# Forgetting attention with a hybrid short convolution: score tiles with keys on partitions in place of transposing P

## The chip, the cores and the metric

The kernel runs on one core of a Trainium2 chip. The time is the device time of one execution in microseconds. Three runs of the kernel before took 593.88, 595.31 and 597.03 us; their median is 595.31.

## The reference

One layer on 1040 positions (16 meta tokens and 1024 real ones), width 1024. A normalised input goes through one projection, whose columns are q, k, v (8 heads of 64 each), a forget logit per head, a gate z, and four groups of 512 columns for a gated convolution. The attention is what the change touches:

```python
log_f = jax.nn.log_sigmoid(f_logit + b_f)
cum_logf = jnp.cumsum(log_f, axis=1)
s = einsum('bqhd,bkhd->bhqk', q, k) * DH ** -0.5
s = s + c_query - c_key                      # c is cum_logf of the head
s = jnp.where(key_pos <= t, s, -inf)
p = softmax(s, axis=-1)
attn = einsum('bhqk,bkhd->bqhd', p, v)
y_attn = group_rmsnorm(attn, attn_norm_g, 8) * silu(z_attn)
y_conv = group_rmsnorm(gate_b * conv3(gate_c * xc), conv_norm_g, 8) * silu(z_conv)
out = rmsnorm(h + concat(y_attn, y_conv) @ w_out)
```

`group_rmsnorm` divides each head by the root of its mean square plus EPS.

## The kernel before

All matmuls are in fp32r. A float32 operand is split into a leading part (a cast to fp32r) and the rest (a subtraction), and a product is summed from leading x leading, leading x rest and rest x leading.

The program has three parts. First come q, k and v for all heads and the cumulative log-forget gates; q, k (each as leading part and rest), v and the gates' negative sums go to DRAM (`qd`, `kd`, `vd`, `cd`). Then comes the attention loop, with the other projections woven in. Last comes the output projection (L788) with the final norm.

The attention loop has 17 stages, -1 to 15 (L716). Stage g computes the scores for one half c (512 queries) of a head, and finishes the half whose scores the stage before made. Per head the half c=1 comes first, then c=0, so even stages finish c=1 (9 key tiles of 128, the last of 16 keys) and odd stages finish c=0 (5 key tiles).

- **`load_head`** (L576) brings q1, q2, k1, k2, v2 of a head into one of two sets of buffers. q1 holds q's leading part above its rest, k1 the leading part of k twice, q2 the leading part and two rows of ones, k2 the rest of k and the two rows of the gates.
- **`s_step`** (L597) takes 128 queries on the partitions and a piece of keys on the columns (`SCH`, 14 pieces per head), in two matmuls, L605 with K=128 and L606 with K=66. VectorE takes the negated maximum of the piece (L612, or L609 with the causal mask on the last piece); ScalarE writes the exponential to `pn` in SBUF with the sum beside it (L613).
- **`s_end`** (L616) combines the pieces' maxima and sums on POOL, ScalarE and VectorE into factors, and POOL scales all of P in SBUF (L635).
- **`t_step`** (L638) makes one key tile of P with keys on the partitions: up to four 128x128 transposes on TensorE into `pt` (L645), a small VectorE transpose for a corner of 32 (L649, L651), a ScalarE cast to `ph` (L654) and a VectorE subtraction to `pl` (L115).
- **`v_step`** (L662), three key tiles behind (`V_LAG`), multiplies `ph` and `pl` with v2 into `po` (L669). `fold` (L672) adds its two halves into `o`; `norm` (L402) normalises and gates.

What sets the order: each step has a place between 0 and 1 in its stage (`S_AT`, `T_AT`, `V_END`), the stage is sorted by place, and `weave` (L745) puts projection blocks (`block_steps`, three matmuls on L165 a step) between the steps in proportion to their estimated length. The matmuls of the loop are pinned: TensorE runs them in exactly this order. The other engines' instructions are ordered by a scheduler at build time. All loads and stores go through SyncE's queue, in order. Tiles of a pool with `bufs=n` rotate over n buffers, and a new tile waits until the old one's readers are done.

## Time and profile before

| | us |
|---|---|
| median of three runs | 595.31 |
| the profiled execution | 596.83 |
| its span in the profile | 595.1 |
| TensorE busy with matmuls | 578.0 (97% of the span, 3230 matmuls) |
| TensorE's weight loads | 509.6 (86%) |
| VectorE | 377.9 (64%) |
| ScalarE | 285.4 (48%) |
| POOL | 168.0 (28%) |
| chain that ended last | 71% TensorE, 10% DMA, 6% VectorE, 4% POOL, 3% ScalarE |

The busy time of a matmul includes time in which the next one already runs, so the sum of durations is not the time that a group of matmuls takes. The attention loop's scores begin at 167.7 us, its first transposes of P at 185.8 us and its last product with V at 490.9 us; the output projection begins at 493.8 us. The profile's PE is TensorE, DVE VectorE, ACT ScalarE, SP SyncE and its queue SPq.

### The profile page before, as it was taken

The numbers are of one execution on the slowest core, as the hardware profiler recorded it, in microseconds if no ns is written. First come the engines' busy times: TensorE is split into PE (matmuls) and PEld (weight loads), VectorE is DVE, ScalarE is ACT, GpSimd is POOL, SyncE is SP. The second block draws the span as 40 slices with busy tenths as digits, with TensorE's granted clock in tenths as the row PEclk, the third lists the DMA queues.
The fourth block names the chain that finished last, engine by engine and source line by source line (L and its number), as shares of the span: only waits on it lengthen the run. The fifth ranks groups of instructions, "written<-read, shape, count | busy, mean of one in ns | idle before, by whom it ended". The sixth has DMA issues, their size and how long they took to land.

```text
span 595.1 us, 9156 instructions
## 1 busy us (share of the span) xinstructions
PE 578.0 (97%) x3230; PEld 509.6 (86%) x3230; DVE 377.9 (64%) x834; ACT 285.4 (48%) x667; POOL 168.0 (28%) x290
## 2 busy tenths in 40 slices
PE   9999999999998999999999999999999999899995
PEld 6888999999997889988879997889998887688884
DVE  5415851133367686879776888868869777947432
ACT  5355431131044575556764655747636676705221
POOL 1002010121027244151243254430552416710000
PEclk9999999999999999999999999999999999899999
DMA  8764594249811605415126134251350227453201
GB/s 287 237 194 141 195 341 142 70 147 280 262 39 36 144 35 135 120 57 155 44 75 143 71 108 112 75 143 37 111 197 16 73 88 243 171 205 113 100 35 70
DMA packets 35221, 78.14 MB, mean 131 GB/s; under 512 B 4024, under 2 KB 13384, under 8 KB 35176
## 3 DMA queue, kind: packets, MB, share of 16 engines
q1 hardware_dynamic: 35032, 77.57, 41.6%
q8 instruction: 25, 0.41, 0.3%
q14 instruction: 20, 0.16, 0.1%
q10 hardware_dynamic: 144, 0.00, 0.0%
HBM read 55.92 MB, written 21.64 MB: 130 GB/s over the span
## 4 chain that ended last, share of the span: by engine, by line
PE 71%; DMA 10%; DVE 6%; POOL 4%; ACT 3%; issue 3%; SPq 2%; POOLq 0%; ACTq 0%; DVEq 0%
PE pj L165 30%; PE ps L324 8%; PE p L788 8%; PE pt L645 5%; PE po L669 5%; PE pj L788 4%; PE ps L165 4%; DMA k<-kd 3%; DMA ht<-in_h 3%; PE pn L605 3%; PE pn L606 3%; DMA xs<-in_hT 2%; DVE mlo L115 2%; POOL pn L635 1%; DMA wm<-in_w_m 1%
## 5 line engine op out<-in xcount | busy, mean ns | idle before, releaser
L165 PE MATMUL pj<-xhi,wmhi 128*128 128x512 f32 (+1 forms) x384 | 144.9, 377 | 1.0 <-DVE kf L275 0.5
L165 PE MATMUL pj<-xhi,wmlo 128*128 128x512 f32 (+1 forms) x384 | 137.1, 357 | 0.0
L165 PE MATMUL pj<-xlo,wmhi 128*128 128x512 f32 (+1 forms) x384 | 136.8, 356 | 0.0
L613 ACT ACTIVATE pn<-pn,nmx 128x328 f32<-128x328 f32 (+6 forms) x112 | 60.5, 541 | 52.7 <-DVE nmx L612 27.9
L165 PEld LDWEIGHTS pj<-xhi,wmlo 128*128 128x128 f32 x384 | 72.2, 188 | 8.4
L165 PEld LDWEIGHTS pj<-xhi,wmhi 128*128 128x128 f32 x384 | 72.6, 189 | 6.2 <-issue 1.4
L165 PEld LDWEIGHTS pj<-xlo,wmhi 128*128 128x128 f32 x384 | 72.8, 190 | 3.8
L654 ACT CAST ph<-pt 128x512 fp32r<-128x512 f32 (+4 forms) x112 | 49.6, 445 | 51.0 <-PE po L669 23.3
L635 POOL TENSOR_SCALAR pn<-pn,fc 128x328 f32<-128x328 f32 (+4 forms) x112 | 69.3, 639 | 1.6
L115 DVE TENSOR_TENSOR pl<-pt,ph 128x512 fp32r<-128x512 f32 (+1 forms) x96 | 54.6, 572 | 20.2 <-ACT ph L654 19.5
L112 POOL TENSOR_SCALAR wmhi<-wm 128x1024 fp32r<-128x1024 f32 x24 | 26.2, 1093 | 141.2 <-DMA wm<-in_w_m 81.8
L645 PE MATMUL pt<-ident,pn 128*128 128x128 f32 x288 | 47.4, 273 | 3.9 <-POOL pn L635 2.2
L645 PEld LDWEIGHTS pt<-ident,pn 128*128 128x128 f32 x288 | 36.3, 140 | 14.4 <-POOL pn L635 3.6
L115 DVE TENSOR_TENSOR wmlo<-wm,wmhi 128x1024 fp32r<-128x1024 f32 x24 | 29.4, 1223 | 18.0 <-POOL wmhi L112 17.9
L609 DVE CUSTOM_DVE_ANT_0 pn<-pn,maskn 128x328 f32<-128x328 f32 (+3 forms) x64 | 31.9, 500 | 11.0 <-PE pn L606 9.3
L669 PE MATMUL po<-ph,v 128*128 128x512 f32 (+4 forms) x112 | 37.0, 336 | 0.0
L605 PE MATMUL pn<-k,q 128*128 128x328 f32 (+6 forms) x112 | 36.6, 328 | 0.1
L606 PE MATMUL pn<-k,q 66*128 66x328 f32 (+6 forms) x112 | 36.1, 322 | 0.0
L669 PE MATMUL po<-pl,v 128*128 128x512 f32 (+1 forms) x96 | 33.2, 350 | 0.0
L788 PE MATMUL p<-whi,mlo 128*128 128x512 f32 (+1 forms) x77 | 30.2, 392 | 2.4 <-DVE mlo L115 2.4
L165 PE MATMUL ps<-xhi,wmhi 128*128 128x346 f32 (+1 forms) x96 | 31.0, 323 | 1.1 <-ACT qraw L240 1.1
L612 DVE TENSOR_REDUCE nmx<-pn 128x1 f32<-128x346 f32 (+4 forms) x48 | 24.8, 521 | 9.6 <-PE pn L606 9.6
(227 smaller groups left out, 1229.5 us busy)
## 6 DMA issues: line engine op xcount, KB each, us to landing
wm<-in_w_m SPq DMA_DIRECT2D x24, 512.0 KB, 3.8
k<-kd SPq DMA_DIRECT2D x24, 260.0 KB, 5.3
q<-qd SPq DMA_DIRECT2D x24, 256.0 KB, 5.9
vd<-vv SPq DMA_DIRECT2D x9, 512.0 KB, 2.9
v<-vd SPq DMA_DIRECT2D x8, 576.0 KB, 6.5
ht<-in_h SPq DMA_DIRECT2D x8, 512.0 KB, 5.6
yd<-gy SPq DMA_DIRECT2D x16, 256.0 KB, 2.8
q<-in_w_o SPq DMA_DIRECT2D x8, 512.0 KB, 4.5
```

The costliest lines, as they stand in the source:

```text
L115: nc.vector.tensor_tensor(lo, src, f(hi), ALU.subtract)
L165: ins = nc.tensor.matmul(ps[:, :w], wt[:, k, :], xt[:, t0:t0 + w], start=(k == 0 and n == 0), stop=(k == KT - 1 and n == 2))
L324: nc.tensor.matmul(ps[c][:P if n == P else 48, :260], x[k][:, ts_] if n == P else x[:, k, :], w[k][:, 260 * c:260 * c + 260], start=(k == ...
L605: pinned(nc.tensor.matmul(ps[:, :w], q1[:, qs], k1[:, ks], start=True, stop=False))
L606: pinned(nc.tensor.matmul(ps[:, :w], q2[:DH + 2, qs], k2[:DH + 2, ks], start=False, stop=True))
L609: nc.vector.tensor_tensor_reduce(ps[:, :w], ps[:, :w], maskn[:, MASKW - w:], op0=ALU.add, op1=ALU.min, scale=-1.0, scalar=-NEG, accum_out= ...
L613: nc.scalar.activation(pn[j][:, ks], ps[:, :w], AF.Exp, bias=nmx[c][at], scale=-1.0 if last else 1.0, accum_out=smx[c][at])
L635: nc.gpsimd.tensor_scalar(pn[j][:, k0:k0 + w], pn[j][:, k0:k0 + w], fc[:, j % 4, i:i + 1], 1.0, ALU.mult, ALU.mult)
L645: pinned(nc.tensor.transpose(pt[:, q0:q0 + P], pn[j][:, ks], ident))
L654: nc.scalar.copy(ph[:, at:], pt[:, at:])
L669: pinned(nc.tensor.matmul(po[:, at:], v2[:, vk, :], t[:, at:], start=(kt == 0 and i == 0), stop=(kt == 4 * c + 4 and i == len(parts) - 1)))
L788: ins = nc.tensor.matmul(held[n][:, :w], a[:, tt], b[:, cs], start=(e == ORDER[0] and i == 0), stop=(e == ORDER[-1] and i == 2))
```

## The change

Per half of a head the maxima now come from one matmul (K=66: leading part of q times leading part of k, plus the gates), and nothing else is made from those scores. `s_end` takes the maximum over the pieces and splits it into two parts; a new `s_row` turns these into a row (transpose on TensorE, ScalarE copy, DMA to `md` in DRAM, DMA back into two rows of q1). `t_step` computes the scores again, this time all terms, with keys on the partitions and queries on the columns: k2 holds the leading part and the rest of k, q2 the rest and the leading part of q (K=128, L665), and k1 times q1 adds leading x leading, the gates and the negated maximum (K=68, L666). The causal mask is a minimum with `maskt` in PSUM (L670), the exponential goes to `pf` in SBUF, and cast and subtraction read `pf`. P isn't normalised: POOL adds up the tiles `pf` in a running sum (L686), `fold` adds the sum's halves, and `norm` gets the sum over keys with two matmuls and adds its square, times EPS, to the mean square. PSUM goes from three buffers for `pn` and two for `pt` to two and three. The build sets a smaller scratch area for DMA descriptors.

Of the diff, the parts below; imports, comments and the unused lines of the old code are left out.

```diff
+    md = [dram.tile([8, P], F32, name=f"md{i}") for i in range(2 * HEADS)]
...
+    maskt = const.tile([P, P], F32, name="maskt")
...
-    psn = cp.enter_context(tc.tile_pool(name="psn", bufs=3, space=PSUM, reuse_waits="tile"))
-    pst = cp.enter_context(tc.tile_pool(name="pst", bufs=2, space=PSUM, reuse_waits="tile"))
+    psn = cp.enter_context(tc.tile_pool(name="psn", bufs=2, space=PSUM, reuse_waits="tile"))
+    pst = cp.enter_context(tc.tile_pool(name="pst", bufs=3, space=PSUM, reuse_waits="tile"))
...
-    def norm(y, g, z, res):
+    def norm(y, g, z, res, s=None):
...
+        if s is not None:
+            th = own.tile([P, 512], F32R, name="gth")
+            tl = own.tile([P, 512], F32R, name="gtl")
+            nc.scalar.copy(th, s)
+            lo_vec(tl, s, th)
...
         def rest():
+            if s is not None:
...
+                pinned(nc.tensor.matmul(pd, blk, th, start=True, stop=False))
+                pinned(nc.tensor.matmul(pd, blk, tl, start=False, stop=True))
+                d2 = own.tile([P, 512], F32, name="gd2")
+                nc.scalar.activation(d2, pd, AF.Square, scale=DH * EPS ** 0.5)
...
+                nc.vector.tensor_add(res, pm, d2)
+                nc.scalar.activation(res, res, AF.Ln)
...
+    ROW = 0.12
...
-        nc.gpsimd.memset(f(q2[DH:DH + 2, :]), 1.0)
+        nc.gpsimd.memset(f(q1[DH:DH + 4, :]), 1.0)
+        nc.gpsimd.memset(f(k1[DH:DH + 4, :]), 1.0)
         nc.sync.dma_start(f(q1[0:DH]), qd[m][0, es, :])
         nc.sync.dma_start(f(k1[0:DH]), kd[m][0, es, :])
...
     def s_step(hd, j, i):
...
-        pinned(nc.tensor.matmul(ps[:, :w], q1[:, qs], k1[:, ks], start=True, stop=False))
-        pinned(nc.tensor.matmul(ps[:, :w], q2[:DH + 2, qs], k2[:DH + 2, ks], start=False, stop=True))
+        pinned(nc.tensor.matmul(ps[:, :w], q1[:DH + 2, j * P:j * P + P], k1[:DH + 2, k0:k0 + w],
+                                start=True, stop=True))
...
-        nc.scalar.activation(pn[j][:, ks], ps[:, :w], AF.Exp, bias=nmx[c][at], scale=-1.0 if last else 1.0,
-                             accum_out=smx[c][at])
...
-    def s_end(c):
+    def s_end(c, box):
         mx = pnp.tile([P, 4], F32, name="mx")
         nc.vector.tensor_reduce(mx, nmx[c], AX.X, ALU.min)
...
+        box["mx"] = pnp.tile([P, 8], F32R, name="mx2")
+        nc.vector.tensor_copy(box["mx"][:, 0:4], mx)
+        lo_vec(box["mx"][:, 4:8], mx, box["mx"][:, 0:4])
...
+    def s_row(hd, c, box):
+        ps = psn.tile([P, 512], F32, name="pn")
+        pinned(nc.tensor.transpose(ps[:8, :P], f(box["mx"]), ident))
+        mr = pnp.tile([8, P], F32, name="mr")
+        nc.scalar.copy(mr, ps[:8, :P])
+        nc.sync.dma_start(md[2 * hd + c], mr)
+        q1 = heads[hd][0]
+        nc.sync.dma_start(f(q1[DH + 2:DH + 4, 512 * c:512 * c + 512]),
+                          md[2 * hd + c].rearrange("(r j) p -> r (j p)", r=2))
...
+    def t_step(hd, c, kt, box):
...
-            pinned(nc.tensor.transpose(pt[:, q0:q0 + P], pn[j][:, ks], ident))
...
+        pinned(nc.tensor.matmul(pt[:rs.stop, a0:], k2[:, ks], q2[:, qs], start=True, stop=False))
+        pinned(nc.tensor.matmul(pt[:rs.stop, a0:], k1[:DH + 4, ks], q1[:DH + 4, qs], start=False, stop=True))
+        pf = pp.tile([P, 512], F32, name="pf" if kt else "ps", bufs=3 if kt else 2)
+        if kt >= 4 * c:
+            new = pt[rs, a0:min(at + P, 512)]
+            nc.vector.tensor_tensor(new, new, maskt[rs.start:rs.stop, a0 - at + r0:a0 - at + r0 + new.shape[-1]], ALU.min)
+        nc.scalar.activation(pf[rs, a0:], pt[rs, a0:], AF.Exp)
...
+            nc.scalar.copy(ph[:, a0:], pf[:, a0:])
+            lo_vec(pl[:, a0:], pf[:, a0:], ph[:, a0:])
...
+        if kt == 0:
+            box["sum"] = pf
+        else:
+            nc.gpsimd.tensor_tensor(box["sum"][rs, a0:], box["sum"][rs, a0:], pf[rs, a0:], ALU.add)
...
     def fold(hd, c, box):
...
+        nc.scalar.copy(tmp[a], box["sum"][b])
+        nc.gpsimd.tensor_tensor(sums[m, c][a], box["sum"][a], tmp[a], ALU.add)
...
+            steps.append((hi + ROW, 0.0, lambda hd=hd, c=c, mbox=mbox: s_row(hd, c, mbox)))
```

The order moves at three places. The first is TensorE at the end of stage -1, where the first key tile of head 0 begins. L605 and L606 are the two old score products, L645 the transposes of P, L165 (L170 in the change) the projection, L646 the new row transpose, L626 the new score product, L665 and L666 the two products of a key tile. Before:

```order
L165 MATMUL pj<-xlo_112,wmhi 128x512
L165 MATMUL pj<-xhi_111,wmlo 128x512
L605 MATMUL pn<-k_1634,q_1632 128x272 [waits Activation_49]
L606 MATMUL pn<-k_1635,q_1633 128x272
L645 MATMUL pt<-ident,pn_1623 128x128 [waits Pool_49]
L645 MATMUL pt<-ident,pn_1622 128x128
```

Changed:

```order
L170 MATMUL pj<-xhi_132,wmlo 128x512
L646 MATMUL pn<-ident,mx_1869 8x128 [waits DVE_49]
L626 MATMUL pn<-k_1643,q_1641 128x144
L626 MATMUL pn<-k_1643,q_1641 128x272 [waits Activation_49]
L170 MATMUL pj<-xhi_134,wmhi 128x512
L170 MATMUL pj<-xlo_135,wmhi 128x512
L170 MATMUL pj<-xhi_134,wmlo 128x512
L665 MATMUL pt<-q_1642,k_1644 128x512 [waits DMAHW3_49,DMAHW4_49,DMAHW1_49,DMAHW0_49]
L666 MATMUL pt<-q_1641,k_1643 128x512 [waits DMAHW4_49]
```

Where the transposes waited for POOL, the second product of the first key tile now waits for a DMA, with six matmuls between it and the row transpose.

The second is SyncE's queue at the first change of head. `md3` is the row of head 1, half c=1; q1_1918 is q1 of head 1, q1_2332 and k1_2334 belong to head 2, whose buffers head 0 leaves. Changed:

```order
L138 DMA wm_2382<-in_w_m 128x1024 [waits DMAHW5_49,DMAHW0_49,DVE_49]
L610 DMA q2_2333<-qd1_64 64x1024 [waits PE_49]
L649 DMA md3_76<-mr_2291 8x128 [waits Activation_49]
L607 DMA q1_2332<-qd1_64 64x1024 [waits DMAHW7_49,DMAHW4_49,PE_49]
L608 DMA k1_2334<-kd1_68 64x1040
L651 DMA q1_1918<-md3_76 2x512 [waits DMAHW2_49]
L609 DMA k1_2334<-cd_72 2x1040 [waits Pool_49]
```

The row's way out and back (L649, L651) has loads of head 2 before and between, and these wait for TensorE. Two more of the seven changes of head have two large loads between the two as well.

The third is VectorE beside POOL in the finish of one half. L120 is `lo_vec`, L670 the mask, L438 and L439 the norm. VectorE, changed:

```order
L670 TENSOR_TENSOR pt<-pt,maskt 128x128 [waits PE_49]
L438 TENSOR_TENSOR gy<-gy,cv 128x512 [waits Activation_49]
L439 SCALAR_TENSOR_TENSOR gy<-gy,gct,zc 128x512 [waits DVE_49]
L120 TENSOR_TENSOR pl<-pf,ph 128x272 [waits Activation_49]
L670 TENSOR_TENSOR pt<-pt,maskt 128x128 [waits PE_49]
L120 TENSOR_TENSOR pl<-pf,ph 128x144 [waits Activation_49]
```

POOL, changed (L686 the running sum, L714 the fold, L674 a memset, L117 the cast of a weight tile):

```order
L117 TENSOR_SCALAR wmhi<-wm 128x1024 [waits DMAHW2_49,PE_49,Pool_49]
L686 TENSOR_TENSOR ps<-ps,pf 128x512 [waits Activation_49,Pool_49] x3
L686 TENSOR_TENSOR ps<-ps,pf 128x400 [waits Activation_49,Pool_49]
L686 TENSOR_TENSOR ps<-ps,pf 128x272 [waits Activation_49,Pool_49]
L686 TENSOR_TENSOR ps<-ps,pf 128x144 [waits Activation_49,Pool_49]
L674 MEMSET ph 128x16 [waits DVE_49,PE_49]
L686 TENSOR_TENSOR ps<-ps,pf 16x16 [waits Activation_49,Pool_49]
L714 TENSOR_TENSOR osum<-ps,stmp 64x512 [waits Pool_49]
```

The subtractions read `pf` and `ph`; POOL's additions read the same `pf` and the running sum, one for each key tile but the first.

## Rows read from the trace of the kernel before

**Rows 1.** Windows view: busy time and count per engine, granted clock, DMA share.

```profile
190.00:490.00 300.00, 297.25 (x1663) 261.14 (x1661) 232.65 (x575) 179.71 (x456) 109.59 (x203) 1.00 0.33 96
```

**Rows 2.** TensorE's timeline: start, duration, line, operation, output<-inputs, shapes, count.

```profile
186.97 0.60 PE L645 MATMUL pt<-ident,pn 128*128 128x128 f32 x4
187.32 0.47 PE L165 MATMUL pj<-xhi,wmhi 128*128 128x512 f32 x1
187.63 0.39 PE L165 MATMUL pj<-xlo,wmhi 128*128 128x512 f32 x1
187.86 0.39 PE L165 MATMUL pj<-xhi,wmlo 128*128 128x512 f32 x1
```

**Rows 3.** The same, end of prologue; in brackets idle time, its releaser.

```profile
182.93 0.23 PE L605 MATMUL pn<-k,q 128*128 128x144 f32 x1
...
183.10 0.44 PE L165 MATMUL pj<-xhi,wmhi 128*128 128x512 f32 x1
...
183.84 0.28 PE L605 MATMUL pn<-k,q 128*128 128x272 f32 x1
183.97 0.28 PE L606 MATMUL pn<-k,q 66*128 66x272 f32 x1
185.76 0.66 PE L645 MATMUL pt<-ident,pn 128*128 128x128 f32 x4 [1.51 <-POOL pn L635]
```

**Rows 4.** The same view, a product of 32 columns.

```profile
205.23 0.22 PE L669 MATMUL po<-ph,v 128*128 128x32 f32 x1
205.30 0.48 PE L165 MATMUL pj<-xhi,wmhi 128*128 128x512 f32 x1
```

**Rows 5.** Waits of the weight loads: us in total, times, longest.

```profile
PEld pt L645 <- POOL pn L635: 3.6, 4, 1.7
```

**Rows 6.** The page's groups: busy us, mean ns | idle before, releaser.

```profile
L645 PE MATMUL pt<-ident,pn 128*128 128x128 f32 x288 | 47.4, 273 | 3.9 <-POOL pn L635 2.2
...
L115 DVE TENSOR_TENSOR wmlo<-wm,wmhi 128x1024 fp32r<-128x1024 f32 x24 | 29.4, 1223 | 18.0 <-POOL wmhi L112 17.9
...
L606 PE MATMUL pn<-k,q 66*128 66x328 f32 (+6 forms) x112 | 36.1, 322 | 0.0
```

**Rows 7.** DMA issues: count, size, median us from issue to landing.

```profile
yd<-gy SPq DMA_DIRECT2D x16, 256.0 KB, 2.8
...
out<-q SPq DMA_DIRECT2D x6, 256.0 KB, 2.3
```

**Rows 8.** SyncE's timeline: an issue among other loads, one by itself.

```profile
196.18 0.59 SPq L586 DMA_DIRECT2D k<-kd  x1
...
513.85 0.33 SPq L692 DMA_DIRECT2D yd<-gy  x1
```

**Rows 9.** TensorE's timeline, output projection: the longest wait.

```profile
517.21 0.59 PE L788 MATMUL p<-whi,mlo 128*128 128x512 f32 x1 [2.11 <-DVE mlo L115]
```

**Rows 10.** Windows view, the 3.7 us behind that wait.

```profile
517.20:520.90 3.70, 3.69 (x9) 2.92 (x10) 3.70 (x2) 0.96 (x2) 3.70 (x2) 0.54 0.74 262
```

**Rows 11.** POOL's timeline at the start of the output projection.

```profile
490.98 2.60 POOL L552 TENSOR_TENSOR wlo<-q,whi 128x1024 fp32r<-128x1024 f32 x1 [12.60 <-ACT whi L549]
493.54 3.38 POOL L552 TENSOR_TENSOR v<-q,whi 128x1024 fp32r<-128x1024 f32 x1
```

**Rows 12.** VectorE's timeline in the same stretch.

```profile
491.88 2.78 DVE L115 TENSOR_TENSOR mlo<-k,mhi 128x1024 fp32r<-128x1024 f32 x1 [0.57 <-ACT mhi L549]
494.69 0.69 DVE L478 TENSOR_TENSOR zs<-pj,rbc 128x512 f32<-128x512 f32 x1
495.30 2.71 DVE L115 TENSOR_TENSOR mlo<-k,mhi 128x1024 fp32r<-128x1024 f32 x1
```

**Rows 13.** Groups by line and shape: busy us, mean ns | idle, releaser.

```profile
L115 DVE TENSOR_TENSOR pl<-pt,ph 128x512 fp32r<-128x512 f32 x48 | 32.9, 686 | 14.2 <-ACT ph L654 14.0
...
L654 ACT CAST ph<-pt 128x512 fp32r<-128x512 f32 x48 | 27.8, 582 | 18.4 <-PE po L669 10.6 <-PE pt L645 7.8
...
L115 DVE TENSOR_TENSOR gsl<-gy,gsh 128x512 fp32r<-128x512 f32 x16 | 13.0, 812 | 4.0 <-ACT gsh L407 3.9
```

More of the change, by code (lines that the diff above doesn't have):

```diff
@@ L565, in hybrid_kernel @@
     FAST = 0.5
-    pn = [pnp.tile([P, (j + 1) * P + 32], F32, name=f"pn{j}") for j in range(8)]
-    nmx, smx = [], []
+    nmx = []
     for c in range(2):
         nmx.append(pnp.tile([P, 4, 3], F32, name=f"nmx{c}"))
-        smx.append(pnp.tile([P, 4, 3], F32, name=f"smx{c}"))
         nc.gpsimd.memset(nmx[c], -NEG)
-        nc.gpsimd.memset(smx[c], 0.0)
     def load_head(hd):
@@ L597, in s_step @@
     def s_step(hd, j, i):
-        q1, q2, k1, k2, _ = heads[hd]
+        q1, _, k1, _, _ = heads[hd]
         c = j // 4
@@ new lines, in t_step @@
+    def t_step(hd, c, kt, box):
+        q1, q2, k1, k2, _ = heads[hd]
+        end = kt == 4 * c + 4
+        at = kt * P - NM - 512 * c
+        a0 = max(at, 0)
+        qs = slice(512 * c + a0, 512 * c + 512)
+        r0 = DH if end and c == 0 else 0
+        rs = slice(r0, r0 + NM) if end else slice(0, P)
+        ks = slice(kt * P - r0, kt * P + (NM if end else P))
+        pt = pst.tile([P, 512], F32, name="pt")
+        pinned(nc.tensor.matmul(pt[:rs.stop, a0:], k2[:, ks], q2[:, qs], start=True, stop=False))
[5 more added lines that the diff above has]
+        nc.scalar.activation(pf[rs, a0:], pt[rs, a0:], AF.Exp)
+        ph = pp.tile([P, 512], F32R, name="ph")
+        if end:
+            nc.gpsimd.memset(f(ph[:, a0:]), 0.0)
+            nc.scalar.copy(ph[rs, a0:], pf[rs, a0:])
+            lo_vec(ph[r0 + 32:r0 + 32 + NM, a0:], pf[rs, a0:], ph[rs, a0:])
+            box[kt] = a0, 8, (ph,)
+        else:
+            pl = pp.tile([P, 512], F32R, name="pl")
+            nc.scalar.copy(ph[:, a0:], pf[:, a0:])
+            lo_vec(pl[:, a0:], pf[:, a0:], ph[:, a0:])
+            box[kt] = a0, kt, (ph, pl)
+        if kt == 0:
+            box["sum"] = pf
+        else:
+            nc.gpsimd.tensor_tensor(box["sum"][rs, a0:], box["sum"][rs, a0:], pf[rs, a0:], ALU.add)
@@ L681, in fold @@
         nc.vector.tensor_tensor(o[a, 512 * c:512 * c + 512], po[a], tmp[a], ALU.add)
+        if (m, c) not in sums:
+            sums[m, c] = own.tile([P, 512], F32, name="osum", bufs=3)
+        tmp = own.tile([P, 512], F32, name="stmp")
+        nc.scalar.copy(tmp[a], box["sum"][b])
+        nc.gpsimd.tensor_tensor(sums[m, c][a], box["sum"][a], tmp[a], ALU.add)
     def attn_finish(m, c):
@@ L687, in go @@
             y = own.tile([P, 512], F32, name="gy", bufs=2)
-            rest = norm(outs[m, "o"][:, cs], gat[:, m:m + 1], zsil[m][:, cs], y)
+            rest = norm(outs[m, "o"][:, cs], gat[:, m:m + 1], zsil[m][:, cs], y, sums.pop((m, c)))
             def end():
@@ L702, in finish_soon @@
             attn_finish(*soon.pop(0))
-    for j in range(8):
-        nc.gpsimd.memset(pn[j][:, (j + 1) * P + NM:], 0.0)
     def spread(steps, todo, lo, hi):
```

68 lines of the change are left out of this document (20 added, 48 removed).

## Prediction

> **What bounds the kernel now.** I read the busy shares first, then TensorE's own order in time, then who it waits for, then the engines that would take over. In the stretch from 190 to 490 us, which is the attention loop, TensorE is busy 297 of 300 us and VectorE, the next engine, 233 [rows 1]. Busy time of pipelined matmuls says little by itself, so I go by the distance from one start to the next. Full-width projection matmuls start 0.23 us apart, and four transposes take 0.35 us and push the matmul behind them 0.08 further out, so 0.107 each [rows 2]. Two score products of 144 columns take 0.17 together and one of 272 takes 0.13 [rows 3]; one of 32 columns takes 0.07 [rows 4]. Columns and starts therefore set the pace, with few gaps: the weight loads of the transposes waited for POOL's scaling 3.6 us in all [rows 5], 1.5 of it at the very first one, at 184 us [rows 3]. TensorE is the bound. VectorE has 67 idle microseconds in those 300, and POOL 190 [rows 1].
>
> **The change, TensorE's own work.** Per head both versions sweep 4736 columns of scores, in 14 pieces, 338 columns on average, which is 0.16 us a piece between the prices of 272 and 512 columns.
> - The second product of the row-wise scores goes: 112 x 0.16 [rows 6] = -17.9.
> - The transposes of P go: 288 x 0.107 [rows 2, 6] = -30.8.
> - Added are two products for each key tile. Each head has six of 512 columns, two each of 400, 272, 144 and 16. With 0.185 for 400 (between 272 and 512), 0.085 for 144 and 0.07 for 16 (the row of 32 columns), that is 2.34 us, times two products, times 8 heads = +37.4.
> - The products with V lose 16 columns in the narrow tiles: -0.6. The norm's new matmuls, 8 x 2 x 0.23 = +3.7. Sixteen row transposes at 0.107 = +1.7.
>
> Sum: -6.5 us. "No transposes" saves little because the transposes were cheap and are replaced by a second full set of scores.
>
> **Waits that go.** No matmul waits for POOL's scaling of P any more: -3.6 [rows 5].
>
> **The wait that comes: the row of maxima.** The maximum crosses from queries on partitions to a row through a transpose on TensorE, a ScalarE copy, a DMA to DRAM and a DMA back into q1. The second product of the first key tile reads that row, its place on TensorE is fixed, and all projection matmuls queue behind it. The trace of before has no such pair of small transfers. Its bounds are the fastest and a typical write, 2.3 and 2.8 us to landing [rows 7], each twice, with 0.33 to issue each [rows 8] and 0.3 for transpose and copy: 5.5 to 6.5, and I take 6.0. What TensorE has to do meanwhile I counted from the new order with the distances above. In the prologue it is two score pieces, three projection matmuls and one product: 1.2 us. At the seven changes of head (SyncE's piece of the order shows one) it is 4.8 to 6.3, 5.25 on average. At the eight changes inside a head it is about 10 us, which covers it; if SyncE is held up there by 4 us, that cover is gone too.
> - Prologue: 6.0 - 1.2 = +4.8 (between 4.3 and 5.3). After the 2.1 us wait at 517 us [rows 9] the granted clock was 0.54, the lower level of 1.2 GHz, and nine matmuls took 3.7 us [rows 10], 0.41 each in place of 0.23: another +1.6.
> - Changes of head: 7 x 0.75 = 5.3. In three of them SyncE first issues two large loads, held until TensorE is done with the old head, between the write and the read of the row. Each such issue takes 0.59 [rows 8], so 3 x 1.2 = 3.5 more. Together +8.8, between 0 (chain of 4.8, or gaps that other stalls widen) and 7 x 3 = 21 (the read waits behind the data of those loads too).
>
> **VectorE and POOL.** VectorE loses 64 small transposes and 64 memsets (about 23 us) and 16 reciprocals (3), and gains 80 masks of up to 128 columns (about 21), sixteen full operations in the norm (11) and the splits of the maxima (6): +12 on 233, still inside its idle time. ScalarE trades its accumulator reads for copies and squares, about even, at 180 of 300. POOL trades 112 scalings for 96 adds, and it has room. The danger is that the two meet. POOL's add of 1024 columns takes 2.6 us, and up to 3.4 when VectorE works beside it [rows 11]. A VectorE subtraction with both inputs in SBUF took 2.78 and 2.71 beside it [rows 12], against 1.22 without it [rows 6]; the operation between them, which reads PSUM and one SBUF tile, took its usual 0.69 [rows 12]. Today's 96 subtractions that split P read PSUM and one SBUF tile. In the change they read pf and ph, both in SBUF, just when POOL adds the same pf.
>
> What this costs VectorE is bounded by two rows. The norm's subtraction, both inputs in SBUF, took 0.81 beside POOL's scalings, against 0.69 for today's split [rows 13]: 0.12 x 96 = 12 us. At the other end, from 491.9 to 498.0 two subtractions took 5.49 for 2.45 of work, an excess of half the time that POOL was adding. POOL's adds are 29.7 thousand columns and the folds 8.2, at 2.5 ns a column 96 us, so 48 us. I take the 12, the nearest case (512 columns, in this loop), and let half of it reach TensorE, since the maxima and the projection outputs queue behind a stalled subtraction and have two PSUM buffers each: +6, with 0 and 48 as ends.
>
> The Trainium skill, page "SBUF — State Buffer", section "Who interferes with whom", says that a VectorE instruction with two SBUF inputs contends with a GpSimd instruction that reads SBUF, and that the one that comes second is blocked for the whole instruction. By that rule the trace agrees [rows 11, 12], and a subtraction ready 0.58 after its exponential [rows 13] would wait out the rest of a 1.2 us add, 0.6 x 48 = 29 us for the full tiles alone; with half of it on TensorE the sum below would be 8 us higher.
>
> Costed at nothing: the loads of a head, eight transfers as before and a stage ahead of their use; the memsets for them, one more per head, which wait on POOL until TensorE has left the old head, with adds behind them; and the fifth to eighth load for the output projection, which now wait for the last scores of head 7. The work on the first two tile pairs, fetched earlier, covers these; without it one such transfer shows.
>
> **Sum.** The profiled execution took 596.8 us: 596.8 - 6.5 - 3.6 + 4.8 + 1.6 + 8.8 + 6.0 = 607.9. It ran 1.5 above the median of the runs, so **606 us**, 1.8% slower.
>
> **Rivals.**
> - *The row comes in time and the adds hide* (faster). If write and read take 4.5 us, the seven changes of head cost nothing; VectorE's 67 idle microseconds swallow its excess. For it: VectorE idles 14 us before the full-width splits alone, waiting for ScalarE's casts [rows 13], so some slack is there. Against it: the write lands no faster than 2.3 in any row. It decides at 4.8 us for the chain. Time: 596.8 - 10.1 + 3.3 + 1.6 - 1.5 = 590; without the prologue's wait and the clock behind it 585.
> - *VectorE becomes the bound.* With 48 us of excess it needs 233 + 12 + 48 = 293 of 300; if half of its idle time stays, because it waits for others, the loop takes 327, 27 more: 596.8 - 10.1 + 6.4 + 27 - 1.5 = 619, and with every change of head at 3 us 640. For it: each split meets its own add. Against it: POOL is idle two thirds of the time, so adds do not pile up.
> - *It cancels* (no change). The changes of head cost half, the adds nothing: 596.8 - 10.1 + 6.4 + 4.4 - 1.5 = 596. This is also where the time lies if the new products merely take the place of the old ones.
>
> **How the numbers follow.** The forecast has 0.44, the faster rival 0.26, VectorE as the bound 0.14, cancelling 0.16. A measurement of this kernel tells about 0.5% (3 us) from no change. So faster is 0.26, same 0.16, slower 0.58. The range of 586 to 626 takes in all of the middle, most of the faster rival and the lower part of VectorE's; the forecast by itself is 599 to 616.
>
> **What would show it.** Right: the first product with the row waits 4 to 6 us for a DMA near 182 us and the clock drops behind it; several waits of 1 to 3 us at the changes of head; splits of 512 columns above 0.9 us on average; TensorE's distances unchanged. Wrong: no DMA waits on TensorE after the prologue, splits at 0.69, a loop shorter than 300 us (the faster rival); or VectorE busy above 280 of 300 with the waits on its maxima (the second rival).

## The result and the profile after

The changed kernel takes **651.26 us** (median of four runs, 650.38 to 651.84) against 595.19 for the kernel before (593.88 to 597.03): a ratio of 1.094, 95% interval 1.091 to 1.097. The forecast was 606, with 626 as the upper end. The sign was right; instead of the +11 us it is +56. One of the four runs of u_vecsums below, 623.67 us, was a slow one (1.8% above the fastest), and its median is that of the other three.

The busy times, the span and the mean clock of the profiled execution:

```profile
PE 589.5 (91%) x3086; PEld 507.2 (78%) x3086; DVE 424.6 (65%) x818; ACT 290.1 (45%) x587; POOL 199.9 (31%) x226
core 0: 650.0 us, clock 0.978
```

The same stretch of the loop as in [rows 1], with the columns span, TensorE, weight loads, VectorE, ScalarE, POOL, clock, DMA share and GB/s:

```profile
190.00:490.00 300.00, 260.66 (x1308) 221.73 (x1306) 236.13 (x468) 154.78 (x323) 127.93 (x133) 0.96 0.28 80
```

VectorE is busy 236 of 300 us, after 233 before, and POOL 128 after 110; neither is near full. TensorE is emptier, 261 after 297. What TensorE waited for from 150 us to the end (reason: total us, times, longest):

```profile
PE pn L646 <- DVE mx L120: 15.1, 8, 5.0
PE pt L666 <- DMA q<-md: 7.6, 4, 2.6
PE po L695 <- DVE ph L120: 7.4, 7, 1.7
PE pj L430 <- ACT gd L428: 6.1, 5, 3.3
PE pj L170 <- DVE gy L435: 3.3, 2, 2.9
PE pj L431 <- DVE gsl L120: 2.8, 1, 2.8
...
PE pm L430 <- ACT gd L428: 1.7, 2, 1.0
...
PE po L695 <- DVE pl L120: 0.7, 2, 0.4
```

The kernel before has about 7 us of such waits there, none longer than 2.1. Adding up TensorE's distances beyond the prices of [rows 2 to 4] gives 79 us of waits and slow stretches after, 22 before; its own work, priced alike, is 8 us less. That makes +57 - 8 = 49 of the 55 us between the two profiled executions; the other 6 lie in distances too small to count one by one.

Of the 79 us, 52 are the waits of this view (with the lines that are not shown) and some 10 are matmuls at the lower level of TensorE's clock. The granted clock is 0.50 in five stretches before the end, at 228, 283, 385, 478 and 512 us, 27 us together. Four of them come right behind a wait of TensorE (2.61, 2.77, 3.28 and 2.50 us), and the one at 385 begins in a wait of 5.00; behind the wait of 3.51 at 360 us there is none. In the columns of above:

```profile
385.40:392.20 6.80, 4.56 (x13) 3.69 (x14) 4.39 (x7) 1.69 (x5) 1.95 (x2) 0.50 0.02 6
```

The waits have three roots. The row of maxima: 15.1 at its transpose, 7.6 at its transfer. The norm: 6.1 and 1.7 for ScalarE's square of the denominators, 2.8 for the split of the squares, 3.3 for a buffer that the norm holds. And splits of P, above all the 16-column end tile: 7.4.

VectorE's operations by shape (count | busy us, mean ns | idle before):

```profile
L120 DVE TENSOR_TENSOR pl<-pf,ph 128x512 fp32r<-128x512 f32 x32 | 39.7, 1247 | 5.8 <-ACT ph L680 5.8
L120 DVE TENSOR_TENSOR wmlo<-wm,wmhi 128x1024 fp32r<-128x1024 f32 x18 | 28.2, 1564 | 7.7 <-POOL wmhi L117 7.7
L120 DVE TENSOR_TENSOR pl<-ps,ph 128x512 fp32r<-128x512 f32 x16 | 10.9, 684 | 4.4 <-ACT ph L680 4.3
L640 DVE CAST mx<-mx 128x4 fp32r<-128x4 f32 x16 | 5.1, 320 | 0.2
```

The split of P into `pl` takes 1247 ns where POOL adds beside it, and 684 for the first key tile (`ps`), which POOL does not add. The split of the weights takes 1564 in place of 1223 [rows 6].

One place shows how these join, VectorE from 382 us (start, length, instruction):

```profile
382.20 0.15 DVE L638 TENSOR_REDUCE mx<-nmx 128x4 f32<-128x12 f32 x1
382.28 1.27 DVE L483 SCALAR_TENSOR_TENSOR cv<-cx,cwt,cv 128x1024 f32<-128x1024 f32 x1
383.47 1.23 DVE L640 CAST mx<-mx 128x4 fp32r<-128x4 f32 x1
...
384.81 1.27 DVE L484 SCALAR_TENSOR_TENSOR cv<-cx,cwt,cv 128x1024 f32<-128x1024 f32 x1
386.00 1.51 DVE L120 TENSOR_TENSOR pl<-pf,ph 128x512 fp32r<-128x512 f32 x1
387.44 0.15 DVE L120 TENSOR_TENSOR mx<-mx,mx 128x4 fp32r<-128x4 f32 x1
```

POOL in the same stretch, and TensorE behind it (the last bracket is idle time and its releaser):

```profile
383.13 1.54 POOL L686 TENSOR_TENSOR ps<-ps,pf 128x512 f32<-128x512 f32 x1 [3.72 <-ACT pf L671]
385.63 1.33 POOL L686 TENSOR_TENSOR ps<-ps,pf 128x400 f32<-128x400 f32 x1 [0.97 <-ACT pf L671]
```

```profile
387.64 0.37 PE L646 MATMUL pn<-ident,mx 128*8 128x128 f32 x1 [5.00 <-DVE mx L120]
388.67 0.63 PE L170 MATMUL pj<-xhi,wmhi 128*128 128x512 f32 x1
389.10 0.63 PE L170 MATMUL pj<-xlo,wmhi 128*128 128x512 f32 x1
```

The maximum of a half (L638) is ready at 382.3. Its cast of four columns (L640), 0.15 to 0.17 us in twelve of the sixteen halves, takes 1.23: it ends as POOL's addition ends. Two convolution steps of 1.2 us and one blocked split of 1.5 stand between, and the rest (the second `mx`) comes at 387.5. TensorE, at the transpose L646 in its fixed order, has waited 5.00 us. Behind it matmuls start 0.43 apart, where 0.23 is usual; the granted clock there is 0.50, the lower level.

### The profile page after: what moved, and what is told of

The parts are those of the page before. It is cut to its first block, busy times and chain, and to the rows that moved or that the text cites. A ratio compares the mean times of both kernels' runs of the same rounds, so it can differ in the third digit from the quotient of the medians.

```text
span 650.0 us, 8751 instructions
## 1 busy us (share of the span) xinstructions
PE 589.5 (91%) x3086; PEld 507.2 (78%) x3086; DVE 424.6 (65%) x818; ACT 290.1 (45%) x587; POOL 199.9 (31%) x226
## 4 chain that ended last, share of the span: by engine, by line
PE 57%; DVE 25%; DMA 6%; ACT 6%; issue 3%; POOL 2%; SPq 0%; POOLq 0%; ACTq 0%; DVEq 0%
PE pj L170 14%; PE ps L329 8%; PE p L820 7%; PE ps L170 7%; PE ps L237 6%; DVE pl L120 6%; PE pj L820 4%; PE po L695 3%; DVE wmlo L120 2%; DVE gy L439 2%; DMA q<-md 2%; DMA wm<-in_w_m 2%; DVE pn L630 2%; PE pn L626 2%; PE pt L666 2%
## 5 line engine op out<-in xcount | busy, mean ns | idle before, releaser
L686 POOL TENSOR_TENSOR ps<-ps,pf 128x512 f32<-128x512 f32 (+2 forms) x96 | 94.0, 980 | 178.5 <-ACT pf L671 143.0
L170 PE MATMUL pj<-xhi,wmhi 128*128 128x512 f32 (+1 forms) x384 | 141.3, 368 | 3.8 <-DVE gy L435 3.3
L170 PE MATMUL pj<-xhi,wmlo 128*128 128x512 f32 (+1 forms) x384 | 139.4, 363 | 0.0
L170 PE MATMUL pj<-xlo,wmhi 128*128 128x512 f32 (+1 forms) x384 | 139.2, 362 | 0.0
L170 PEld LDWEIGHTS pj<-xhi,wmhi 128*128 128x128 f32 x384 | 74.3, 193 | 13.4 <-DVE gy L435 4.1
L170 PEld LDWEIGHTS pj<-xhi,wmlo 128*128 128x128 f32 x384 | 73.8, 192 | 8.7
L170 PEld LDWEIGHTS pj<-xlo,wmhi 128*128 128x128 f32 x384 | 74.3, 193 | 6.5
L120 DVE TENSOR_TENSOR pl<-pf,ph 128x512 fp32r<-128x512 f32 (+3 forms) x80 | 68.7, 871 | 15.0 <-ACT ph L680 14.7
L671 ACT ACTIVATE pf<-pt 128x512 f32<-128x512 f32 (+2 forms) x96 | 40.5, 424 | 65.7 <-DVE pt L670 43.3
L117 POOL TENSOR_SCALAR wmhi<-wm 128x1024 fp32r<-128x1024 f32 x24 | 26.7, 1113 | 109.7 <-DMA wm<-in_w_m 77.3
L120 DVE TENSOR_TENSOR wmlo<-wm,wmhi 128x1024 fp32r<-128x1024 f32 x24 | 35.5, 1478 | 14.9 <-POOL wmhi L117 14.8
L666 PE MATMUL pt<-q,k 68*128 68x512 f32 (+4 forms) x112 | 38.2, 341 | 7.6 <-DMA q<-md 7.6
L626 PE MATMUL pn<-k,q 66*128 66x328 f32 (+6 forms) x112 | 37.3, 343 | 4.0 <-DVE nmx L630 2.0
L680 ACT CAST ph<-pf 128x512 fp32r<-128x512 f32 (+3 forms) x80 | 39.6, 500 | 1.6
L665 PE MATMUL pt<-q,k 128*128 128x512 f32 (+4 forms) x112 | 36.6, 327 | 0.0
L666 PEld LDWEIGHTS pt<-q,k 68*128 68x128 f32 (+1 forms) x112 | 20.7, 185 | 13.5 <-DMA q<-md 9.4
L170 PE MATMUL ps<-xhi,wmhi 128*128 128x346 f32 (+1 forms) x96 | 30.9, 322 | 0.0
L695 PEld LDWEIGHTS po<-ph,v 128*128 128x128 f32 x112 | 21.6, 193 | 11.9 <-DVE ph L120 9.1
L170 PE MATMUL ps<-xlo,wmhi 128*128 128x346 f32 (+1 forms) x96 | 30.8, 321 | 0.0
```

What stands on the lines that cost most here:

```text
L120: nc.vector.tensor_tensor(lo, src, f(hi), ALU.subtract)
L170: ins = nc.tensor.matmul(ps[:, :w], wt[:, k, :], xt[:, t0:t0 + w], start=(k == 0 and n == 0), stop=(k == KT - 1 and n == 2))
L626: pinned(nc.tensor.matmul(ps[:, :w], q1[:DH + 2, j * P:j * P + P], k1[:DH + 2, k0:k0 + w], start=True, stop=True))
L666: pinned(nc.tensor.matmul(pt[:rs.stop, a0:], k1[:DH + 4, ks], q1[:DH + 4, qs], start=False, stop=True))
L671: nc.scalar.activation(pf[rs, a0:], pt[rs, a0:], AF.Exp)
L680: nc.scalar.copy(ph[:, a0:], pf[:, a0:])
```

## The experiments

Two theories stood before the experiments. **P**: POOL's sums and VectorE block each other in SBUF, and a late VectorE makes all the waits. **O**: TensorE's fixed order holds new round trips, which are late on an idle VectorE too. The table has every run; "ratio" is to the kernel before, with its 95% interval, and the last column is the difference to the change's 651.3. The intervals of p_sums_unread, d_psumsplit and c_normearly overlap with the change's (1.091 to 1.097): these three are not told apart from it. In the expectations the waits of the change are somewhat longer (16.5 and 8.3 us in place of 15.1 and 7.6, and 8.9 for the square in place of 6.1 + 1.7); they lie between those of the matmuls, shown above, and those of the weight loads ahead of them (17.4, 9.4 and 10.7).

| run | us | ratio | to the change |
|---|---|---|---|
| a_noadds | 631.1 | 1.060 (1.054 to 1.065) | -20 |
| p_sums_unread | 650.2 | 1.091 (1.086 to 1.095) | -1 |
| d_psumsplit | 646.9 | 1.088 (1.081 to 1.094) | -4 |
| j_inplace | 646.6 | 1.087 (1.084 to 1.090) | -5 |
| b_norow | 640.3 | 1.076 (1.071 to 1.082) | -11 |
| g_nomax | 618.0 | 1.038 (1.036 to 1.040) | -33 |
| e_neither | 609.7 | 1.024 (1.020 to 1.027) | -42 |
| h_nodenom | 639.0 | 1.071 (1.066 to 1.077) | -12 |
| i_three | 590.8 | 0.991 (0.989 to 0.994) | -61 |
| c_normearly | 655.4 | 1.100 (1.095 to 1.106) | +4 |
| f_onerow | 638.8 | 1.072 (1.070 to 1.075) | -12 |
| k_onerow_inplace | 620.7 | 1.045 (1.042 to 1.048) | -31 |
| l_endfirst | 633.4 | 1.065 (1.063 to 1.068) | -18 |
| m_all | 633.5 | 1.066 (1.062 to 1.071) | -18 |
| n_onerow_inplace_norm | 613.3 | 1.028 (1.023 to 1.033) | -38 |
| q_onerow_inplace_nodenom | 605.8 | 1.017 (1.011 to 1.023) | -45 |
| u_vecsums | 614.5 | 1.033 (1.026 to 1.040) | -37 |
| t_shift_vecsums | 587.6 | 0.985 (0.980 to 0.991) | -64 |

### POOL's sums

**a_noadds** takes out the additions.

```diff
-        else:
-            nc.gpsimd.tensor_tensor(box["sum"][rs, a0:], box["sum"][rs, a0:], pf[rs, a0:], ALU.add)
```

> Leaves out POOL's running sums of the exponentials (the sums that divide the output are then those of the first key tile alone); all else stays. Theory P (VectorE and POOL block each other in SBUF): the 32 full-width splits of P fall from 1247 ns to about 690, the 1024-column splits of the weights from 1564 to about 1220, VectorE comes in time again for the maxima, the end tiles and the norms, and most of the 57 us of new waits on TensorE go: 610 us or less. Theory O (TensorE's fixed order now holds new round trips, the maxima through three VectorE steps, a transpose and two transfers, and the denominators of the norm, which are late on an idle VectorE too): 635 to 645 us, the waits on the maxima, the row and the norm stay.

631 us: below O's number and far above P's. The full-width splits are as P said (those of the first key tile take 979 ns here, where they take 684 in the change):

```profile
L120 DVE TENSOR_TENSOR pl<-pf,ph 128x512 fp32r<-128x512 f32 x32 | 21.8, 690 | 6.6 <-ACT ph L680 6.6
...
L640 DVE CAST mx<-mx 128x4 fp32r<-128x4 f32 x16 | 2.8, 174 | 0.1
```

Taken shape by shape, VectorE's operations are some 38 us longer in the change than here, 17.9 of it in the full-width splits. But the waits at the transpose and at the row's transfer stay:

```profile
PE pn L646 <- DVE mx L120: 9.7, 8, 3.1
PE pt L666 <- DMA q<-md: 7.5, 5, 2.6
```

Both theories are half right.

**p_sums_unread** keeps the additions and takes away whoever waits for them:

```diff
-            nc.gpsimd.tensor_tensor(box["sum"][rs, a0:], box["sum"][rs, a0:], pf[rs, a0:], ALU.add)
+            dm = pp.tile([P, 512], F32, name="dm", bufs=1)
+            nc.gpsimd.tensor_tensor(dm[rs, a0:], pf[rs, a0:], pf[rs, a0:], ALU.add)
```

> POOL makes the same 80 additions of pf in the same sizes, but into a tile that nobody reads; the sums that fold and norm use are those of the first key tile. Without the additions the time was 631. If they cost by blocking VectorE: 647 to 653, splits of 512 columns above 1150 ns. If fold and norm wait for them: 630 to 638, though the splits are as slow as in the change.

650.2 us, with the full-width splits at 1100 ns:

```profile
L120 DVE TENSOR_TENSOR pl<-pf,ph 128x512 fp32r<-128x512 f32 x32 | 34.9, 1100 | 6.3 <-ACT ph L680 6.3
```

So it is not a wait for the sums that costs 20 us; the additions cost that merely by running. That they do so through VectorE fits the traces (in the loop no wait of TensorE names POOL), but the time does not follow the length of VectorE's operations: they are 25 us longer than in a_noadds here and 38 in the change, at the same time.

**d_psumsplit** and **j_inplace** take one of VectorE's two SBUF inputs away instead.

```diff
@@ d_psumsplit @@
-            lo_vec(pl[:, a0:], pf[:, a0:], ph[:, a0:])
+            nc.scalar.activation(pt[:, a0:], pt[:, a0:], AF.Exp)
+            lo_vec(pl[:, a0:], pt[:, a0:], ph[:, a0:])
@@ j_inplace @@
-        pf = pp.tile([P, 512], F32, name="pf" if kt else "ps", bufs=3 if kt else 2)
...
+        pf = pp.tile([P, 512], F32, name="ps", bufs=2) if kt == 0 else pt
...
-            nc.gpsimd.tensor_tensor(box["sum"][rs, a0:], box["sum"][rs, a0:], pf[rs, a0:], ALU.add)
+            nc.gpsimd.tensor_tensor(box["sum"][rs, a0:], box["sum"][rs, a0:], f(ph[rs, a0:]), ALU.add)
```

> The split of P subtracts from a second exponential in PSUM instead of pf in SBUF: one input in SBUF instead of two, POOL's sums stay. ScalarE gains 64 exponentials (about 32 us on 26 of every 50), the PSUM buffers of the second products are held about 1.5 us longer. Theory P: splits of 512 columns at 690 ns beside the sums, VectorE 25 us less busy: 615 to 632 us. Theory O: no gain, 648 to 660 us.

> The exponential stays in PSUM (but for the first key tile), cast and subtraction read it there, and POOL adds the leading part ph instead of pf; ScalarE has no operation more than in the change. The sums take the leading parts alone. If the blocking between VectorE's splits and POOL's sums is what the sums cost (20 us in the run without them): splits of 512 columns at 690 ns beside 96 sums and 631 to 638 us. If the sums cost by POOL's queue or the buffers instead, or if the longer hold of the PSUM buffers eats it: 645 to 652.

In both the splits are back at 683 to 685 ns beside the same additions, here in j:

```profile
L120 DVE TENSOR_TENSOR pl<-pt,ph 128x512 fp32r<-128x512 f32 x32 | 21.8, 685 | 9.3 <-ACT ph L680 9.2
```

In j the excess over a_noadds is 8 us in place of 38, and still only 5 us come back. So the duration of VectorE's operations alone does not give the time: where the three steps of the maximum still queue on VectorE, TensorE waits there nearly as before (12.6 us at the transpose, 7.0 at the transfer). And the 8 us by which all its waits fall are in good part taken back by matmuls at the lower clock (the table under e_neither). j also holds the PSUM buffers longer, with a new wait of 1.6 us at L665 for `pl`; what the blocking alone is worth is therefore not shown.

### The row of maxima

**b_norow** returns from `s_row` at once; q1's two rows get the gates' sums, loaded with the head.

```diff
+        nc.sync.dma_start(f(q1[DH + 2:DH + 4, :]), cd[:, hd, NM:NM + S])
...
     def s_row(hd, c, box):
+        return
```

> Leaves out the way of the maxima to a row (transpose, copy, two transfers); the exponent is shifted by the gates' running sum, loaded with the head, and by a constant in its place. First products and maxima are still computed, POOL's sums stay. The waits that name this way are 16.5 us (transpose behind the split maxima), 8.3 (second product behind the transfer) and 1.1, and the lower clock behind them. Theory O: these go, 26 us and some 8 us of clock: 612 to 622 us. Theory P: VectorE is as late as before, the waits move to the end tiles, the norms and the projection's outputs: 635 us or more.

640.3, P's number. The row's 23 us of waits are gone; among what is left, `pl` now has 6.6 where it had 0.7, and `gtl` 5.2 where there was no wait:

```profile
PE po L691 <- DVE ph L122: 7.8, 5, 2.9
PE po L691 <- DVE pl L122: 6.6, 9, 1.5
...
PE pj L428 <- DVE gtl L122: 5.2, 1, 5.2
```

Of the 23 us, 10 have moved, to the products with V and to the norm; all waits of TensorE together are 38 us in place of 52.

**e_neither** is a and b together.

> Leaves out both POOL's running sums and the way of the maxima to a row; first products and maxima stay. The two left out alone gave -20 and -11 us. If they are separate costs they add up: 651 - 31 = 620 us. If both are one thing, a late VectorE that TensorE's fixed order meets at the next place when the first is taken away, then without the sums VectorE is in time at those places too, and the whole of the row's 26 us comes back: 651 - 20 - 26 = 605 us or less.

609.7: -42, where a and b alone give -20 and -11. That looks like one lateness that shows at the next place of TensorE's order, and part of it is: with the sums 10 of the row's 23 us of waits move elsewhere, without them 3.5 of 18. But the waits as a whole add up. The table takes the profiled executions apart from 165 us on: TensorE's waits, then what matmuls that start at a granted clock of 0.50 take beyond the prices of [rows 2 to 4], which is an estimate from these prices. The last column is the mean granted clock of the four runs.

| run | waits, us | extra at the lower clock, us | granted clock |
|---|---|---|---|
| the change | 52 | 10 | 0.972 to 0.978 |
| a_noadds | 36 | 9 | 0.981 to 0.990 |
| b_norow | 38 | 13 | 0.965 to 0.973 |
| e_neither | 22 | 4 | 0.988 to 0.994 |
| c_normearly | 51 | 17 | 0.958 to 0.970 |
| f_onerow | 39 | 13 | 0.970 to 0.976 |
| j_inplace | 44 | 16 | 0.965 to 0.970 |
| k_onerow_inplace | 27 | 6 | 0.980 to 0.986 |

Sums and row left out alone take 16 and 14 us off the waits, together 30. What is more than the sum, 11 us of time in these executions, lies for some 8 us in the matmuls at the lower clock: b has more of them than the change, e has less. Why the clock is lower more often in b, though TensorE waits less there, is not shown.

**g_nomax** is b with a `return` at the head of `s_step` and `s_end` too: no first products, no maxima.

> Leaves out the row, the first products and the maxima on VectorE (64 pairs, about 65 us of VectorE); POOL's sums stay. TensorE's own work falls by 112 x 0.16 = 18 us against the run without the row (640). If TensorE's places and not VectorE's load set the time: 622. If VectorE's load does: below 605, with the splits of 512 columns still above 1100 ns.

618.0, 22 us below b, of which 18 are TensorE's own by the prices. VectorE loses 65 us of work and next to nothing comes of it: its **load does not set the time**. That refutes P in its simple form, VectorE as the bound.

**f_onerow** sends the maximum in one rounded part, and the two VectorE steps between L638 and the transpose fall away:

```diff
-        box["mx"] = pnp.tile([P, 8], F32R, name="mx2")
-        nc.vector.tensor_copy(box["mx"][:, 0:4], mx)
-        lo_vec(box["mx"][:, 4:8], mx, box["mx"][:, 0:4])
+        box["mx"] = pnp.tile([P, 4], F32, name="mx")
+        nc.vector.tensor_reduce(box["mx"], nmx[c], AX.X, ALU.min)
...
```

> The maximum goes to a row in one rounded part (a shift need not be exact, only the same for every key): the cast and the subtraction on VectorE fall away between the maximum and its transpose, one row is sent in place of two. Nothing is left out of the result. If the three queued VectorE steps make the 16.5 us wait at the transpose, two thirds of it go: 638 to 644 us. If VectorE is late as a whole, the wait goes on at the row's transfer and behind it: 646 to 652.

638.8, within the first case. The wait at the transpose is 2.9 us in place of 15.1, and 2.6 at the transfer, while the end tile's waits grow to 10.5:

```profile
PE pn L643 <- DVE mx L638: 2.9, 4, 1.3
```

It gains as much as leaving the whole row out did (b; the intervals overlap), and leaves nothing out.

### The norm's denominators

**c_normearly** puts the two products and the square 2.1 us of work ahead of the products for the mean square.

```diff
-        def rest():
+        def pre():
             if s is not None:
...
+                return d2
+        def rest(d2=None):
```

> The two products for the norm's denominators and their square stand 2.1 us of work earlier in TensorE's order than the products for the mean square; nothing is left out. Waits that name this place: 8.9 us on the square, 3.0 on the split of the squares, 3.7 on the sum that frees the PSUM buffer. Theory O: 8 to 12 us faster, 639 to 643. Theory P: 4 us faster at most, since the chain of these waits starts at a late VectorE.

655.4, no gain; the +4 is inside the intervals. The waits on the square go, others take their place (3.4 for the projection's output, 3.3 for a cast in the output projection), and the transpose still has 15.3. All waits are 51 us, 1 less than in the change, and the matmuls at the lower clock take 7 more.

**h_nodenom** calls `norm` without the sums:

```diff
-            rest = norm(outs[m, "o"][:, cs], gat[:, m:m + 1], zsil[m][:, cs], y, sums.pop((m, c)))
+            rest = norm(outs[m, "o"][:, cs], gat[:, m:m + 1], zsil[m][:, cs], y)
```

> Leaves out the norm's denominators alone (their split, two products, square and sum); POOL's sums go on and nobody uses their result. With sums and row left out as well this was worth 19 us. If it is a cost of its own: 630 to 635. If it is one of several places where the same lateness shows: 640 to 650, the waits move to the maxima's transpose and the end tiles.

639.0, at the edge of its second case. The waits have moved to the transpose (21.0 after 15.1), though not to the end tiles (7.1 after 7.4):

```profile
PE pn L646 <- DVE mx L120: 21.0, 9, 6.1
PE pt L666 <- DMA q<-md: 7.3, 4, 3.3
PE po L695 <- DVE ph L120: 7.1, 6, 2.0
```

**i_three** is e_neither without the denominators.

> Leaves out POOL's sums, the row, and the norm's denominators (their split, two products, square and sum); first products and maxima stay. If sums, row and denominators are all that is new besides TensorE's own work, the time is that of before less 8.3 us of work and 3.7 of the norm's products, some 585 us, and the waits on TensorE are below 20 us. If the exact T products, the masks and the end tiles bring waits of their own: 595 to 610.

590.8 us, below the kernel before and between its two cases. Its waits are 10 us in all, as the first had it; the longest group, and its loop in the columns of above:

```profile
PE po L689 <- DVE ph L122: 2.6, 4, 1.1
```

```profile
190.00:490.00 300.00, 291.31 (x1496) 250.47 (x1495) 236.10 (x543) 188.65 (x364) 56.66 (x62) 0.99 0.33 94
```

TensorE's excess is 23 us in all, as before the change (22). So the three parts hold the whole loss: sums, row and denominators. What else the change alters (the second full set of scores, masks and end tiles, the PSUM buffers, the smaller area for DMA descriptors) is still there in this run and makes no loss that shows. VectorE is busy 236 us of these 300, the same share as in the change, which takes 60 us longer (the window holds less of the loop there: 1308 matmuls, 1496 here).

### Mending it

**k_onerow_inplace** is f and j together.

> The one rounded row (-12 us alone) and the exponential in PSUM together; the sums take the leading parts alone. If the two work on the same lateness they gain more together than apart, as leaving out sums and row did: 615 to 625. If they are separate: 639 less whatever the exponential in PSUM gains alone. If VectorE's wait for the PSUM buffers is new: 640 or more.

620.7: -31, where f and j alone give -12 and -5. Together more than apart, as with e, and again mostly by the clock: the waits fall by 13 and 8 us alone and by 25 together, while the matmuls at the lower clock take 3 and 6 us more alone and 4 less together.

**l_endfirst** adds the order of key tiles `[0] + list(range(4 * c + 4, max(4 * c - 1, 0), -1)) + list(range(1, 4 * c))`, **m_all** the earlier denominators too.

> As the run before, and the narrow key tiles (16, 144, 272, 400 columns) come second to fifth in a stage's order instead of last, so that the V products of the 16-column tile no longer follow its second products within about 2 us of TensorE's work. The waits on that tile's split (8.7 us in the change, 12.1 with one row) go: 8 to 12 us below the run before. If VectorE's lateness only moves to the next place: within 3 us of it.

> As the run before, and the norm's denominators 2.1 us of work earlier. Alone that made no gain (655) since the waits went to the next place. With VectorE nearer to in time the 8 us of waits on ScalarE's square go: 4 to 8 us below the run before. If they move again: no gain.

Both lose 13 us against k, which neither case for l had; m against l is the second case of m, no gain. The end tile's waits on V are gone, but the row is now waited for, here in l, where k has 2.4 us:

```profile
PE pt L663 <- DMA q<-md: 10.8, 7, 4.4
```

Why the row comes later in this order was not tried. **n_onerow_inplace_norm** therefore has the old order of tiles.

> One rounded row, exponential in PSUM, sums of the leading parts, and the denominators' products 2.1 us of work earlier, in the order of key tiles of the change. The waits on ScalarE's square (7.8 us) and on the split of the denominators (3.8) are what is left to gain against 621: 610 to 615 if VectorE and ScalarE are in time now; 618 to 624 if the waits move again.

613.3: the step that gave no gain in c gives -7 here, 6 of it in waits. **q_onerow_inplace_nodenom** leaves the denominators out:

> One rounded row and exponential in PSUM, without the norm's denominators; POOL's sums go on unread. If the denominators cost 19 us on their own: 600 to 604. If the gain is that of a shared lateness already mended: 608 to 615.

605.8, between its two cases: 15 us for the denominators here, 12 alone (h), 19 with sums and row gone (e to i); 3.7 of each are TensorE's own products.

**u_vecsums** is n with the additions on VectorE, from PSUM. **t_shift_vecsums** is u without first products, maxima and row.

```diff
-            nc.gpsimd.tensor_tensor(box["sum"][rs, a0:], box["sum"][rs, a0:], f(ph[rs, a0:]), ALU.add)
+            nc.vector.tensor_tensor(box["sum"][rs, a0:], pf[rs, a0:], box["sum"][rs, a0:], ALU.add)
```

> One rounded row, exponential in PSUM, denominators' products earlier, and the running sums on VectorE, from PSUM, in place of POOL: nothing is left out, sums of the whole exponentials. VectorE gains 80 additions, about 42 us on 39 of every 50. If what is left of the blocking is worth more than that load: below 610 us. If VectorE's load sets the time at about 88% busy: 620 us or more, with its waits spread over maxima, end tiles and norms.

> As the run before, and without first products, maxima and row: the shift is the gates' running sum and a constant (a shift cancels in the quotient, but nothing guards the exponential against large products any more). TensorE's own work is 596.8 - 8.3 - 17.9 = 571 us with the waits of the kernel before; VectorE loses 65 us. 575 to 590 us if TensorE sets the time, faster than the kernel before; above 595 if VectorE's order still holds it up.

u: 614.5, between its two cases, and its interval takes in n's ratio: moving the additions from POOL to VectorE gains nothing that can be told from no change. t: 587.6, faster than the kernel before by 0.9 to 2.0%. It is no replacement: without the maximum nothing guards the exponential. A version with maximum and denominators that beats the kernel before was not found; n is nearest, 2.8% above it.

## Why the prediction was wrong

The sum has +21 us of new waits, clock and blocking; some 46 us of new waits and 8 of lower clock came. Three steps failed: the chain of the row began at the transpose, with nothing for the VectorE steps in front of it (15.1 us of waits there); the norm was priced by its columns alone, 3.7 us where leaving it out is worth 12 to 19; and the term for VectorE beside POOL was 6 us where leaving the sums out is worth 20.

**TensorE's own work, -6.5: right.** Priced by the same distances it is 8 us less. (The two products of a head are 2.32 us by the prices given and not 2.34, which is 0.3 us in the sum.) **Waits on POOL's scaling, -3.6: right**, none is left.

**"The wait that comes": a part left out, which failed, and two sizes off.** I counted the chain from the transpose on, and took the maximum to be there. In front of it stand three VectorE steps, each queued again behind what the scheduler put between. The chain of waits at the first row shows it:

```profile
177.04 0.07 DVE mx L638
177.12 1.19 DVE cv L483
178.31 0.08 DVE mx L640
178.39 1.24 DVE cv L484
179.63 0.07 DVE mx L120
179.71 1.19 DVE cv L485
180.89 0.61 DVE zc L494
...
181.59 0.63 ACT otmp L455
...
182.24 0.26 ACT mr L648
...
182.52 1.21 DMA md<-mr
...
183.75 1.51 DMA q<-md
...
185.30 0.50 PE pt L666
```

From the maximum to its rest 2.7 us, with two convolution steps of 1.2 between; then ScalarE's copy behind an activation of the gate that itself waited for VectorE. At this first row TensorE's transpose came late enough not to wait. It waited at eight others, all seven changes of head among them: there the rest was done 0.5 to 5.2 us behind the maximum, which is 12 of the 15.1 us; for the other 3 the maximum itself was late. This part was costed at nothing and is the largest wait of all.

The transfers that I did price (4.8 + 1.6 + 8.8) cost less: 1.21 and 1.51 here, 2.7 together, where I had 5.3 to 6.3 with their issue; a wait of 1.4 in place of 4.8, and no lower clock behind it. Of the changes of head, the term 7 x 0.75 did not come: at four of them TensorE does not wait for the transfer. The term 3 x 1.2 had the right cause: the waits come at the three where SyncE issues two large loads between write and read, 2.61, 1.10 and 2.50 us. The first of them, SyncE's queue and TensorE:

```profile
221.41 0.47 SPq L649 DMA_DIRECT2D md<-mr  x1
221.99 0.45 SPq L607 DMA_DIRECT2D q<-qd  x1
222.48 0.60 SPq L608 DMA_DIRECT2D k<-kd  x1
224.56 0.23 SPq L651 DMA_DIRECT2D q<-md  x1
```

```profile
227.30 0.50 PE L666 MATMUL pt<-q,k 68*128 68x512 f32 x1 [2.61 <-DMA q<-md]
```

The pair took 3.14 and 2.69 there. All waits on it: 7.6.

**The clock, +1.6: too small, and in the wrong place.** It did not fall in the prologue. It fell behind later waits, for some 10 us, where the kernel before has some 2.

**"The norm's new matmuls, 8 x 2 x 0.23 = +3.7": the step that failed without a doubt.** It prices the columns alone. The square of the denominators goes through ScalarE's queue and stands right ahead of the next pinned products, one more round trip in a fixed order, eight times. The waits named after the norm are 14 us; leaving the denominators out is worth 12 to 19, that is 8 to 15 beyond the columns.

**"VectorE and POOL", +6, with 0 and 48 as ends: mechanism right for the splits, size wrong.** I took the bound of 12 us from a subtraction beside POOL's scalings as the nearest row and halved it. The excess is some 38, nearer to the other end, which came from subtractions beside POOL's additions [rows 11, 12]: it was the row of the same pair of operations, and against it I held "POOL is idle two thirds of the time". A split and the addition of the same tile are both released by ScalarE within 0.6 us, so most of them meet, however idle POOL is: 26 of the 32 full-width splits took 0.85 us or more, the other six 0.67 to 0.68. On the time the sums cost 20 us alone and 31 with the row gone (b to e).

The estimate by the Trainium skill's rule (page "SBUF — State Buffer", "Who interferes with whom") would have put the forecast 8 us higher, too little as well. It gave 29 us on the full tiles because it counted 48 of them; the first tile of each half has no addition, and 0.6 x 32 = 19 is close to the 18 us that the full-width splits lost. For these splits the trace agrees with the rule.

**The second rival had the place right, not the sign by which to know it.** It asked for VectorE above 280 of 300. VectorE stayed at 236, and TensorE waited for it all the same. Its price, 619 to 640, rested on that share and was too low as well. (The small transposes and memsets that went are 64 x 216 and 64 x 85 ns in the trace of before, 19 us and not 23; that does not change how VectorE's load was judged.) That costs do not add up (20 and 11 make 42, 12 and 5 make 31) was in no case of the prediction; by the estimate under e_neither the clock makes most of that.

## What to carry to other kernels

In an order that is fixed on the engine that bounds, price a new dependency by its whole round trip through the other engines' queues, each step behind one long operation, and not by its own columns or by the busy share of the engine that it crosses. Runs that leave out one of several new waits can show too little: a part of the waits moves on, and here the clock took more back than that. Read the waits and the matmuls at the lower clock apart, and leave causes out in pairs, before you say what each is worth. And take the bound from the row that shows the same two operations side by side.
